# Latent attention and output projection: maxima moved to a rotating bank, first two score groups begun early, output tiles split inside the preceding tile

## The chip, the cores and the metric

The kernel runs on one core of a Trainium2 chip. The metric is the device time of one execution in microseconds (us), as the median of three runs. The core's engines run side by side, each on its own instruction stream in program order: TensorE (PE in the profile, with its weight loads as PEld), VectorE (DVE), ScalarE (ACT), GpSimd (POOL), and SyncE (SP), which here only issues transfers. Engines wait for each other through semaphores. Matrix products land in PSUM, which the program holds as one tile `PB` of eight banks of 128 x 512 words.

## The reference

The reference is a two-layer backbone over 1,024 latent tokens and 256 context tokens with model width 1,024. Layer 0 is windowed attention, layer 1 is latent attention, and a final RMS norm gives the output. The change touches only the end of layer 1:

```
s = (einsum("bqhd,bkhd->bhqk", qn, kn) + einsum("bqhd,bkd->bhqk", qr, kr)) * scale
p = softmax(s, axis=-1)
o = einsum("bhqk,bkhd->bqhd", p, v)          # 16 heads, 64 values each
yx = (o * silu(gx)) @ w_out                  # 1024 x 1024
x = x + gate_x[:, None] * yx
return rms_norm(x, final_g)
```

Only the 1,024 latent tokens are queries here; the keys are all 1,280 tokens.

## The kernel before

**Units.** Attention runs as 16 units (`UnitB`, numbered 0 to 15 by `ui`): eight pairs of heads, each for two halves of 512 queries. Unit `ui` has pair `ui // 2` and half `ui % 2`. Keys come in ten chunks of 128 (`c` = 0 to 9). All instructions from here to the end are in the order in which the program writes them, on every engine; no scheduler moves them.

**Scores.** `score(c)` makes the transposed scores of both heads of the pair for one chunk: 10 matmuls (five terms, two heads; the two heads of a term sit in different halves of the rows) into banks 3 and 4 for even `c`, 5 and 6 for odd `c`. The fifth term (`KR`, part 1, 36 rows) also adds minus the row maximum: rows 32 to 35 of each head's part of `q[:, 3]` hold it. Then ACT takes the exponential of both banks at once (128 x 1024) into a ring of six buffers, and POOL adds it into the running sum `acc` (in unit 15, from `c` = 5, DVE does that).

**Maxima of the next unit.** While unit `ui` runs, `nu.top(PIECES[c])` makes the untransposed scores of unit `ui + 1` in two banks taken in turn from banks 0, 1, 2 (`topb`), and DVE reduces each bank to maxima. At the unit's end, `turn` reduces these and transposes them on PE into bank 5 (`psd`); `shift` writes them into `q[:, 3]`, one head's rows by DVE and the other's by four ACT instructions.

**Values.** `PV` multiplies exponentials and values into bank 7: chunks 0 to 4 at `c` = 5, chunks 5 to 9 at the unit's end. `fin` copies bank 7 out. `fin2` (the sums of `acc` over partitions, four PE passes into bank 5, copied out by ACT), `fin3(0)`, `fin3(1)` (reciprocal and product for 256 queries each) and `fin4` (times the gate, store to `og_d`) of unit `ui` run inside unit `ui + 1`.

**Fills.** At the end of units 0, 2, ..., 12 `make_K` builds the next pair's keys: three pieces of 6 matmuls (512, 512 and 256 wide), each in the next bank of its own turn over banks 0, 1, 2 (`fillb`), split into a high and a low part by ACT and DVE. At the end of units 3, 7 and 11 `make_V` builds values in five pieces of 12 matmuls of 256. Units 1, 5, 9, 13 and 14 have no fill. So the order at a unit's end is: `PV(5, 10)`, `turn`, the previous unit's `fin3(1)`, `shift`, its `fin4`, the fill, `fin`, and then `score(0)` of the next unit.

**Output projection.** `out_tiles` does eight tiles of 128 tokens. `fetch_out` loads a tile's 1024 x 128 attention outputs from `og_d` and its 128 x 1024 residual. `split` makes a high part (ACT copy, 128 x 1024, L121) and a low part (DVE difference, L122). Then come two groups (`c` = 0, 1) of 8 x 3 matmuls of 128 x 512 (L126, L127, L128: high x high, low x high, high x low), in banks 0 to 3 in turn. After each group DVE multiplies by the gate (L1434) and adds the residual (L1435), and ACT sums squares (L1436). POOL makes the norm factor (L1450 to L1452), DVE applies it to both halves (L1463), and SP stores them. `out_tiles` is a generator: it stops three times inside tile 0, and unit 15's `fin2`, `fin3`, `fin4` are put in after the third stop, in the middle of the second group. Tile `ti + 1` is fetched after the first group of tile `ti` (tile 4 at the end of tile 3), and is split at the head of its own tile.

Of the kernel before, what the change touches and what calls it, by code (L numbers as in the profile page):

```python
# [9 lines left out]
F32 = mybir.dt.float32  # L10
F32R = mybir.dt.float32r
BF16 = mybir.dt.bfloat16
AF = mybir.ActivationFunctionType
# [20 lines left out]
class Ring:  # L34
# [6 lines left out]
    def next(self):  # L41
        b = self.bufs[self.i % len(self.bufs)]
        self.i += 1
        return b


def shp(ap, *dims):
    n = 1
    for d in dims:
        n *= d  # L50
    ap = ap[:, 0:n]
    if len(dims) == 1:
        return ap
    names = "abcdefg"[: len(dims)]
    kw = {c: d for c, d in zip(names[1:], dims[1:])}
    return ap.rearrange("p (" + " ".join(names) + ") -> p " + " ".join(names), **kw)
# [3 lines left out]
def kernel(ctx: ExitStack, tc: tile.TileContext, t, out, dbg=None):  # L60
    nc = tc.nc
# [7 lines left out]
    ident = cpool.tile([128, 128], F32, name="ident")  # L69
# [13 lines left out]
    load = nc.sync.dma_start  # L83
# [35 lines left out]
    def split(hi, lo, src, lo_eng=None):  # L119

        nc.scalar.copy(hi, src)  # L121
        (lo_eng or nc.vector).tensor_sub(lo, src, hi.bitcast(F32))  # L122
# [786 lines left out]
    og = None  # L909
# [366 lines left out]
    class UnitB:  # L1276
# [37 lines left out]

        def turn(self):
            nc.vector.reduce_max(shp(self.mx, 2, 64)[:, :, 32:36], self.mxp, AX.X, negate=True)
            nc.tensor.transpose(psd[0:100, 0:128], self.mx[:, 0:100], ident)

        def shift(self, engs):
            for r, eng in zip((slice(32, 36), slice(96, 100)), engs):  # L1320
                if eng is nc.vector:
                    eng.tensor_tensor(
                        shp(self.q[r, 3], 4, 128), psd[r, 0:128].unsqueeze(1).to_broadcast([4, 4, 128]),
                        ident[r, r].unsqueeze(2).to_broadcast([4, 4, 128]), ALU.mult,
                    )
                else:
                    for b in range(4):
                        o = self.q[r, 3, b * 128 : b * 128 + 128]
                        eng.activation(o, psd[r, 0:128], AF.Copy, scale=ident[r, r.start + b : r.start + b + 1])  # L1329

        def score(self, c):


            q, kt = self.q, self.kt
            cs = slice(c * 128, c * 128 + 128)
            b = 3 + 2 * (c % 2)
            for i, (k, s, sq, n) in enumerate(((kt, 0, 0, 64), (kt, 0, 1, 64), (kt, 1, 0, 64), (KR, 0, 2, 64), (KR, 1, 3, 36))):
                for e in range(2):
                    r = slice(64 * e, 64 * e + n)
                    nc.tensor.matmul(PB[:, b + e, :], k[r, s, cs], q[r, sq], start=i == 0, stop=i == 4)  # L1340
            E = self.E[c] = shp(Er.next(), 2, 512)
            nc.scalar.activation(E, PB[:, b : b + 2, :], AF.Exp)  # L1342
            acc = shp(self.acc, 2, 512)
            eng = nc.vector if self.i == NU - 1 and c > 4 else nc.gpsimd
            if c == 1:
                eng.tensor_add(acc, self.E[0], E)
            elif c:
                eng.tensor_add(acc, acc, E)  # L1348

# [22 lines left out]
            nc.vector.reciprocal(self.rec[:, js], self.rec[:, js])  # L1372
            nc.vector.tensor_mul(self.o[:, js], self.o[:, js], self.rec[:, js])

        def fin4(self):
            nc.vector.tensor_mul(self.o, self.o, self.gt.bitcast(F32))
            load(out=og_d[self.pair, :, self.ts], in_=self.o)


    gx1 = R[:, 0:1024].bitcast(F32)  # L1380
# [27 lines left out]
        load(out=x, in_=x1_d[256 + ti * 128 : 384 + ti * 128, :])  # L1408
        return o, x

    def out_tiles(nxt):
        for ti in range(8):
            ts = slice(ti * 128, ti * 128 + 128)
            o, xi = nxt
            x = yr.next()
            og = shp(ogr1.next(), 2, 8, 128)
            split(og[:, 0], og[:, 1], o.bitcast(F32))
            st = sm_ring()
            css = [slice(c * 512, c * 512 + 512) for c in range(2)]
            for c in range(2):  # L1420
                parts = [css[c]] if ti < 7 or c == 0 else [slice(512, 768), slice(768, 1024)]
                for i, cs in enumerate(parts):
                    n = cs.stop - cs.start
                    ps = pso1()
                    for k in range(8):
                        mm3(
                            ps[:, 0:n], [og[:, s, k, :] for s in range(2)], [WoB[k][:, s, cs] for s in range(2)],
                            k == 0, k == 7,
                        )
                        if ti == 0 and k == 3:  # L1430
                            yield
                    if c == 0 and ti < 7 and ti != 3:
                        nxt = fetch_out(ti + 1)
                    nc.vector.tensor_mul(x[:, cs], ps[:, 0:n], gx1[:, cs])  # L1434
                    nc.vector.tensor_add(x[:, cs], x[:, cs], xi[:, cs])  # L1435
                    nc.scalar.activation(junk1[:, 0:n], x[:, cs], AF.Square, accum_out=st[:, c + i : c + i + 1])  # L1436
                    if ti == 7 and c + i < 2:
                        nc.vector.tensor_mul(x[:, cs], x[:, cs], fg[:, cs])
                    if ti == 7 and c + i == 1:
                        nc.vector.tensor_add(st[:, 0:1], st[:, 0:1], st[:, 1:2])  # L1440
                        nc.vector.tensor_scalar(st[:, 0:1], st[:, 0:1], 1.0 / D, EPS, ALU.mult, ALU.add)
                if ti == 0:
                    yield
            r = st[:, 3:4]
            if ti == 3:
                nxt = fetch_out(4)
            if ti == 7:
                nc.vector.scalar_tensor_tensor(st[:, 2:3], st[:, 2:3], 1.0 / D, st[:, 0:1], ALU.mult, ALU.add)
            else:
                nc.gpsimd.tensor_add(st[:, 2:3], st[:, 0:1], st[:, 1:2])  # L1450
                nc.gpsimd.tensor_scalar(st[:, 2:3], st[:, 2:3], 1.0 / D, EPS, ALU.mult, ALU.add)
            nc.gpsimd.tensor_tensor(r, st[:, 2:3], mhalf, ALU.pow)  # L1452
            if ti == 7:
                nc.vector.tensor_scalar_mul(x[:, 0:512], x[:, 0:512], r)
                load(out=out[ts, 0:512], in_=x[:, 0:512])
                nc.scalar.activation(x[:, 512:768], x[:, 512:768], AF.Copy, scale=r)
                cs = slice(768, 1024)
                nc.vector.scalar_tensor_tensor(x[:, cs], x[:, cs], r, fg[:, cs], ALU.mult, ALU.mult)
                load(out=out[ts, 512:1024], in_=x[:, 512:1024])
                continue  # L1460
            for c in range(2):
                cs = css[c]
                nc.vector.scalar_tensor_tensor(x[:, cs], x[:, cs], r, fg[:, cs], ALU.mult, ALU.mult)  # L1463
                load(out=out[ts, cs], in_=x[:, cs])
# [32 lines left out]
    for ui, u in enumerate(units):  # L1497
        pu = units[ui - 1] if ui else None
        nu = units[ui + 1] if ui + 1 < NU else None
        nnu = units[ui + 2] if ui + 2 < NU else None  # L1500
        for c in range(NT):
            if c == 5:
                if pu:
                    pu.fin2()
                u.PV(0, 5)
                if pu:
                    pu.fin3(0)
                if pu and nu is None:
                    pu.fin3(1)
                    pu.fin4()  # L1510
            u.score(c)
            if nu:
                nu.top(PIECES[c])
            if 0 < ui < 12 and c == 2 or ui == 6 and c == 7 or ui in (12, 13) and c in (2, 7):
                next(wo_fill, None)
            if nu is None and c == 0:
                load2(out=gx1, in_=gate_d[1, 0, :].partition_broadcast(128))
                load2(out=fg, in_=t["final_g"].partition_broadcast(128))
        if nnu:
            nnu.prep()  # L1520
        if nu is None:
            nxt = fetch_out(0)
        u.PV(5, NT)
        if nu:
            nu.turn()
            if pu:
                pu.fin3(1)
            nu.shift((nc.vector, nc.scalar))
            if pu:
                pu.fin4()  # L1530
            fill = make_K(u.pair + 1) if u.half == 0 and u.pair < 7 else iter(())
            if ui % 4 == 3:
                fill = make_V(ui // 4 + 1)
            for _ in fill:
                pass
        u.fin()
    out_fill = out_tiles(nxt)
    next(out_fill)
    next(out_fill)
    next(out_fill)  # L1540
    units[-1].fin2()
    units[-1].fin3(0)
    units[-1].fin3(1)
    units[-1].fin4()
    for _ in out_fill:
        pass
    in_order.__exit__(None, None, None)


# [73 lines left out]
```

## Time and profile before

| | us |
|---|---|
| median of three runs | 1640.3 (1639.24 to 1640.78) |
| the profiled execution | 1641.39 |
| its span, first to last instruction | 1639.5 |
| PE busy | 1541.3 (94%) |
| DVE busy | 1008.0 (61%) |
| POOL busy | 776.3 (47%) |
| ACT busy | 733.7 (45%) |
| mean granted TensorE clock | 0.971 |

The profiled execution lies 1.1 us above the median and its span 1.9 us below its own time. The page cuts the span into 40 slices of 41 us and gives one digit for each: busy tenths, or tenths of the full TensorE clock. A timeline row reads: start, duration, engine, line, operation, output <- inputs, shapes, and in square brackets the idle time of the engine before it with the instruction that ended it. Matmul records overlap, since matmuls are pipelined: the step from one start to the next is the cost of one. A row of the view by windows gives, for one stretch, its length, each engine's busy time with its count of instructions, the granted clock, the share of the transfer engines and GB/s.

### The profile page before, as it was taken

What the parts mean: (1) busy time and instruction counts of PE and PEld (TensorE: products, weight loads), DVE (VectorE), ACT (ScalarE), POOL (GpSimd) and SP (SyncE); (2) the same over time, 40 slices, a digit from 0 to 9 for tenths busy, and PEclk for the clock granted to TensorE, in tenths of its full rate; (3) what the DMA queues carried; (4) which work ended last, traced back from release to release, by engine and by line L of the source; (5) the groups of instructions that cost most, each with busy time, mean ns of one, the idle gap of its engine ahead of it and who ended that gap; (6) DMA issues with size and microseconds to landing.
All of it is one profiled execution on the core that took longest, in us unless ns stands there. A gap on an engine that the chain in (4) does not pass through costs nothing.

```text
span 1639.5 us, 24729 instructions
## 1 busy us (share of the span) xinstructions
PE 1541.3 (94%) x9026; PEld 1196.6 (73%) x9026; DVE 1008.0 (61%) x1886; ACT 733.7 (45%) x1425; POOL 776.3 (47%) x722
## 2 busy tenths in 40 slices
PE   6899999989999999998999999999999999997666
PEld 2788788777888888878887887667667667655555
DVE  2666778637777777778263015676776776873232
ACT  2511221248777777776233322444445445441111
POOL 2653356235453333445164503787787777770000
PEclk8899999989999999999999999999999999998877
DMA  8435544573343333253138514011211211212221
GB/s 305 153 123 177 203 151 145 173 187 118 92 139 101 91 91 91 78 160 113 37 116 291 158 55 119 11 52 43 78 56 43 84 43 58 63 54 94 77 82 60
DMA packets 123698, 178.91 MB, mean 109 GB/s; under 512 B 11692, under 2 KB 71724, under 8 KB 123576
## 3 DMA queue, kind: packets, MB, share of 16 engines
q1 hardware_dynamic: 116296, 166.40, 31.9%
q10 hardware_dynamic: 7280, 10.92, 2.2%
q8 instruction: 71, 1.16, 0.3%
q14 instruction: 51, 0.42, 0.1%
HBM read 131.13 MB, written 46.15 MB: 108 GB/s over the span
## 4 chain that ended last, share of the span: by engine, by line
PE 79%; DVE 6%; issue 5%; POOL 4%; ACT 3%; DMA 2%; POOLq 0%; DVEq 0%; SPq 0%; ACTq 0%
PE PB L127 13%; PE PB L126 13%; PE PB L128 13%; PE PB L1340 11%; PE PB L1355 8%; PE PB L570 5%; PE PB L1305 5%; PE PB L560 4%; PE PB L533 2%; PE PB L534 2%; DVE arena_r L122 1%; PE PB L1366 1%; DVE arena_f L344 1%; PE PB L674 1%; POOL arena_r L122 1%
## 5 line engine op out<-in xcount | busy, mean ns | idle before, releaser
L126 PE MATMUL PB<-arena_r 128*128 128x512 f32 (+2 forms) x1312 | 484.0, 369 | 30.8 <-ACT arena_r L121 27.6
L127 PE MATMUL PB<-arena_r 128*128 128x512 f32 (+2 forms) x1312 | 478.0, 365 | 18.7 <-DVE arena_r L122 15.6
L128 PE MATMUL PB<-arena_r 128*128 128x512 f32 (+2 forms) x1312 | 475.9, 363 | 0.2 <-DVE arena_r L122 0.2
L126 PEld LDWEIGHTS PB<-arena_r 128*128 128x128 f32 x1312 | 255.0, 194 | 80.7 <-ACT arena_r L121 32.0
L1348 POOL TENSOR_TENSOR arena_f<-arena_f 128x1024 f32<-128x1024 f32 x123 | 294.5, 2395 | 25.6 <-ACT arena_f L1342 18.4
L127 PEld LDWEIGHTS PB<-arena_r 128*128 128x128 f32 x1312 | 254.2, 194 | 58.0 <-DVE arena_r L122 19.1
L128 PEld LDWEIGHTS PB<-arena_r 128*128 128x128 f32 x1312 | 254.1, 194 | 36.6 <-DVE arena_r L122 0.4
L1311 DVE TENSOR_REDUCE krF<-PB 128x1 f32<-128x512 f32 (+1 forms) x264 | 167.3, 678 | 109.1 <-PE PB L1305 109.1
L1342 ACT ACTIVATE arena_f<-PB 128x1024 f32<-128x1024 f32 x160 | 164.2, 1027 | 150.3 <-PE PB L1340 147.7
L1340 PE MATMUL PB<-arena_r 64*128 64x512 f32 (+1 forms) x1600 | 220.6, 394 | 3.9 <-ACT arena_r L1329 3.2
L122 POOL TENSOR_TENSOR arena_r<-arena_f,arena_r 128x512 fp32r<-128x512 f32 x96 | 132.2, 1389 | 166.6 <-ACT arena_r L121 157.6
L1340 PEld LDWEIGHTS PB<-arena_r 64*128 64x128 f32 (+1 forms) x1600 | 156.1, 184 | 49.6 <-issue 13.3
L122 DVE TENSOR_TENSOR arena_r<-PB,arena_r 128x512 fp32r<-128x512 f32 (+2 forms) x215 | 140.1, 663 | 76.6 <-ACT arena_r L121 75.0
L540 DVE CUSTOM_DVE_ANT_0 arena_f<-PB,arena_f,small 128x256 f32<-128x256 f32 (+1 forms) x288 | 145.4, 524 | 32.6 <-PE PB L534 25.8
L121 ACT CAST arena_r<-PB 128x512 fp32r<-128x512 f32 (+2 forms) x215 | 120.0, 565 | 55.1 <-PE PB L560 40.8
L1355 PE MATMUL PB<-arena_f 128*64 128x512 f32 x640 | 143.6, 595 | 0.0
L541 ACT ACTIVATE arena_f<-arena_f,small 128x640 f32<-128x640 f32 (+2 forms) x160 | 118.9, 743 | 27.9 <-DVE small L540 26.9
L570 PE MATMUL PB<-arena_r 128*128 128x512 f32 x336 | 121.8, 438 | 4.7 <-ACT arena_f L581 4.1
L344 DVE SCALAR_TENSOR_TENSOR arena_f<-arena_f,small 128x512 f32<-128x512 f32 x98 | 115.0, 1219 | 3.9 <-DMA arena_f<-ada_w 3.5
L1305 PE MATMUL PB<-arena_r 64*128 64x512 f32 (+1 forms) x768 | 107.9, 357 | 0.9 <-DVE arena_r L122 0.9
L560 PE MATMUL PB<-ident,arena_f 128*128 128x128 f32 x672 | 105.7, 274 | 0.4 <-ACT arena_f L541 0.3
L1355 PEld LDWEIGHTS PB<-arena_f 128*64 128x64 f32 x640 | 44.4, 137 | 84.2 <-issue 82.0
(165 smaller groups left out, 1886.0 us busy)
## 6 DMA issues: line engine op xcount, KB each, us to landing
arena_r<-q_d SPq DMA_DIRECT2D x148, 128.0 KB, 2.8
arena_f<-ada_w SPq DMA_DIRECT2D x64, 256.0 KB, 3.5
arena_f<-a_w_in SPq DMA_DIRECT2D x40, 256.0 KB, 3.1
arena_f<-ada_w SPq DMA_DIRECT2D x16, 512.0 KB, 7.6
arena_f<-x SPq DMA_DIRECT2D x16, 512.0 KB, 4.2
q_d<-arena_f SPq DMA_DIRECT2D x16, 512.0 KB, 3.1
qn_d<-arena_f SPq DMA_DIRECT2D x16, 512.0 KB, 5.7
arena_r<-qn_d SPq DMA_DIRECT2D x16, 512.0 KB, 5.6
```

What stands on the lines that cost most here:

```text
L122: (lo_eng or nc.vector).tensor_sub(lo, src, hi.bitcast(F32))
L126: nc.tensor.matmul(o, ah, bh, start=first, stop=False)
L127: nc.tensor.matmul(o, al, bh, start=False, stop=False)
L128: nc.tensor.matmul(o, ah, bl, start=False, stop=last)
L560: nc.tensor.transpose(pt[:, h, :], self.Ps[h][:, ci * 128 : ci * 128 + 128], ident)
L570: nc.tensor.matmul(self.pv, V[:, self.chunks[ci], self.g, :], PT[:, s], start=ci == 0 and s == 0, stop=ci == self.m - 1 and s == 1,)
L1305: nc.tensor.matmul(bank[:, o : o + n], self.q[r, s, bs], k[r, 0, n0 : n0 + n], start=s == 0, stop=s == 2)
L1311: nc.vector.reduce_max(self.mxp[:, e, b : b + 1, i], bank[:, 0:n], AX.X)
L1340: nc.tensor.matmul(PB[:, b + e, :], k[r, s, cs], q[r, sq], start=i == 0, stop=i == 4)
L1342: nc.scalar.activation(E, PB[:, b : b + 2, :], AF.Exp)
L1348: eng.tensor_add(acc, acc, E)
L1355: nc.tensor.matmul(PB[r, 7, :], Vq[:, c, h, :], E[:, e], start=c == 0, stop=c == NT - 1)
```

## The change

1. `turn` no longer writes the transposed maxima to bank 5 but to the next bank of `topb` (`self.pm`), and `shift` reads them there.
2. `score` takes a range of terms. At `c` = 0 the unit issues the first four terms of `score(0)` and of `score(1)`, then `top` of chunk 0, then the last term of `score(0)` with its exponential and sum; at `c` = 1 it issues `top`, then the last term of `score(1)`. From `c` = 2 on the order is as before.
3. In unit 15, `fin4` of unit 14 is done in two halves of 256 queries, each stored on its own. The fetch of output tile 0 follows the first half, that of tile 1 the second.
4. `cut_out` is the split of an output tile, in two halves of 512 columns. Tile 0 is cut before unit 15's `fin`; tile `ti + 1` is cut inside tile `ti`, after its first group, and tile `ti + 2` is fetched right behind.
5. `out_tiles` is now an ordinary function, and unit 15's `fin2`, `fin3`, `fin4` stand ahead of it.

```diff
         def turn(self):
             nc.vector.reduce_max(shp(self.mx, 2, 64)[:, :, 32:36], self.mxp, AX.X, negate=True)
-            nc.tensor.transpose(psd[0:100, 0:128], self.mx[:, 0:100], ident)
+            self.pm = topb()
+            nc.tensor.transpose(self.pm[0:100, 0:128], self.mx[:, 0:100], ident)
...
-        def score(self, c):
+        def score(self, c, i0=0, i1=5):
...
+            terms = ((kt, 0, 0, 64), (kt, 0, 1, 64), (kt, 1, 0, 64), (KR, 0, 2, 64), (KR, 1, 3, 36))
+            for i in range(i0, i1):
+                k, s, sq, n = terms[i]
                 for e in range(2):
                     r = slice(64 * e, 64 * e + n)
                     nc.tensor.matmul(PB[:, b + e, :], k[r, s, cs], q[r, sq], start=i == 0, stop=i == 4)
+            if i1 < 5:
+                return
...
-        def fin4(self):
-            nc.vector.tensor_mul(self.o, self.o, self.gt.bitcast(F32))
-            load(out=og_d[self.pair, :, self.ts], in_=self.o)
+        def fin4(self, c0=0, c1=512):
+            cs = slice(c0, c1)
+            nc.vector.tensor_mul(self.o[:, cs], self.o[:, cs], self.gt[:, cs].bitcast(F32))
+            t0 = self.ts.start
+            load(out=og_d[self.pair, :, t0 + c0 : t0 + c1], in_=self.o[:, cs])
...
+    def cut_out(f, eng=None):
+        o, x = f
+        og = shp(ogr1.next(), 2, 8, 128)
+        for h in range(2):
+            hs = slice(4 * h, 4 * h + 4)
+            split(og[:, 0, hs], og[:, 1, hs], o[:, hs].bitcast(F32), eng)
+        return og, x
...
-    def out_tiles(nxt):
+    def out_tiles(ready, got):
         for ti in range(8):
             ts = slice(ti * 128, ti * 128 + 128)
-            o, xi = nxt
+            og, xi = ready
             x = yr.next()
-            og = shp(ogr1.next(), 2, 8, 128)
-            split(og[:, 0], og[:, 1], o.bitcast(F32))
...
-                        if ti == 0 and k == 3:
-                            yield
-                    if c == 0 and ti < 7 and ti != 3:
-                        nxt = fetch_out(ti + 1)
+                    if c == 0 and ti < 7:
+                        ready = cut_out(got)
+                        if ti < 6:
+                            got = fetch_out(ti + 2)
...
                 if pu and nu is None:
+                    pu.fin4(0, 256)
+                    first = fetch_out(0)
                     pu.fin3(1)
-                    pu.fin4()
-            u.score(c)
+                    pu.fin4(256, 512)
+                    got = fetch_out(1)
+            if c == 0:
+                u.score(0, 0, 4)
+                u.score(1, 0, 4)
+            if c > 1:
+                u.score(c)
             if nu:
                 nu.top(PIECES[c])
+            if c < 2:
+                u.score(c, 4, 5)
...
-        if nu is None:
-            nxt = fetch_out(0)
         u.PV(5, NT)
...
+        else:
+            ready = cut_out(first)
         u.fin()
-    out_fill = out_tiles(nxt)
-    next(out_fill)
-    next(out_fill)
-    next(out_fill)
-    units[-1].fin2()
-    units[-1].fin3(0)
-    units[-1].fin3(1)
-    units[-1].fin4()
-    for _ in out_fill:
-        pass
+    u.fin2()
+    u.fin3(0)
+    u.fin3(1)
+    u.fin4()
+    out_tiles(ready, got)
```

More of the change, by code (lines that the diff above doesn't have):

```diff
@@ L1322, in shift @@
                     eng.tensor_tensor(
-                        shp(self.q[r, 3], 4, 128), psd[r, 0:128].unsqueeze(1).to_broadcast([4, 4, 128]),
+                        shp(self.q[r, 3], 4, 128), self.pm[r, 0:128].unsqueeze(1).to_broadcast([4, 4, 128]),
                         ident[r, r].unsqueeze(2).to_broadcast([4, 4, 128]), ALU.mult,
@@ L1328, in shift @@
                         o = self.q[r, 3, b * 128 : b * 128 + 128]
-                        eng.activation(o, psd[r, 0:128], AF.Copy, scale=ident[r, r.start + b : r.start + b + 1])
-        def score(self, c):
+                        eng.activation(o, self.pm[r, 0:128], AF.Copy, scale=ident[r, r.start + b : r.start + b + 1])
+        def score(self, c, i0=0, i1=5):
             q, kt = self.q, self.kt
@@ L1336, in score @@
             b = 3 + 2 * (c % 2)
-            for i, (k, s, sq, n) in enumerate(((kt, 0, 0, 64), (kt, 0, 1, 64), (kt, 1, 0, 64), (KR, 0, 2, 64), (KR, 1, 3, 36))):
+            terms = ((kt, 0, 0, 64), (kt, 0, 1, 64), (kt, 1, 0, 64), (KR, 0, 2, 64), (KR, 1, 3, 36))
+            for i in range(i0, i1):
+                k, s, sq, n = terms[i]
                 for e in range(2):
@@ L1441, in out_tiles @@
                         nc.vector.tensor_scalar(st[:, 0:1], st[:, 0:1], 1.0 / D, EPS, ALU.mult, ALU.add)
-                if ti == 0:
-                    yield
             r = st[:, 3:4]
-            if ti == 3:
-                nxt = fetch_out(4)
             if ti == 7:
```

## The prediction

> **What bounds the kernel now.** I read the page's slices first, then windows by stage, then who waited for whom on PE, then timelines.
>
> ```profile
> span 1639.5 us, 24729 instructions
> ...
> PEclk8899999989999999999999999999999999998877
> ```
>
> ```profile
> 742.70:745.00 2.30, 0.18 (x2) 0.13 (x2) 2.30 (x6) 1.56 (x5) 1.29 (x3) 1.00 0.42 110
> 745.00:750.00 5.00, 3.50 (x27) 3.27 (x28) 4.15 (x7) 4.16 (x11) 4.26 (x5) 1.00 0.24 52
> 1200.00:1300.00 100.00, 99.81 (x727) 69.73 (x724) 72.36 (x94) 48.76 (x67) 74.76 (x34) 1.00 0.17 52
> 1497.40:1516.70 19.30, 14.35 (x48) 10.93 (x48) 5.01 (x7) 2.38 (x5) 0.93 (x3) 0.73 0.29 96
> 1612.50:1632.70 20.20, 14.96 (x72) 12.51 (x72) 7.39 (x13) 2.89 (x7) 0.93 (x3) 0.75 0.07 27
> 1632.70:1639.50 6.80, 0.00 (x0) 0.00 (x0) 1.89 (x5) 1.02 (x3) 0.55 (x1) 0.67 0.21 77
> ```
>
> The clock row shows the tail at once: its last four slices of 41 us read 8, 8, 7, 7. The windows give busy time of PE, PEld, DVE, ACT, POOL, then the granted clock, the transfer share and GB/s. In the units (1200 to 1300) PE is busy all the time at full clock, so whatever makes PE wait there is paid. In the output projection it is not: a tile of 48 matmuls takes 19.3 us (the last one 20.2) at a granted clock of 0.73 to 0.75. The next two views, PE's waits in the tail and then in the units, say for what:
>
> ```profile
> PE PB L126 <- ACT arena_r L121: 25.5, 7, 5.9
> PE PB L127 <- DVE arena_r L122: 14.8, 7, 2.3
> ```
>
> ```profile
> PE PB L1340 <- ACT arena_r L1329: 3.2, 5, 0.7
> PE PB L1340 <- DVE arena_r L1322: 0.5, 1, 0.5
> ```
>
> The tail loses 40.3 us in waits for the split of each tile, seven times both halves. The units lose 3.7 us to the shift, at the five boundaries without a fill. The timeline of one change of tile, PE, then DVE, then ACT:
>
> ```profile
> 1511.55 0.39 PE L128 MATMUL PB<-arena_r 128*128 128x512 f32 x1
> ...
> 1516.31 0.39 PE L128 MATMUL PB<-arena_r 128*128 128x512 f32 x1
> 1519.95 0.80 PE L126 MATMUL PB<-arena_r 128*128 128x512 f32 x1 [3.26 <-ACT arena_r L121]
> 1522.78 0.79 PE L127 MATMUL PB<-arena_r 128*128 128x512 f32 x1 [2.03 <-DVE arena_r L122]
> 1523.38 0.63 PE L128 MATMUL PB<-arena_r 128*128 128x512 f32 x1
> 1523.80 0.63 PE L126 MATMUL PB<-arena_r 128*128 128x512 f32 x1
> ```
>
> ```profile
> 1516.73 0.69 DVE L1434 TENSOR_TENSOR arena_f<-PB,arena_r 128x512 f32<-128x512 f32 x1 [4.02 <-PE PB L128]
> 1517.46 0.69 DVE L1435 TENSOR_TENSOR arena_f<-arena_f,arena_r 128x512 f32<-128x512 f32 x1
> 1520.18 1.41 DVE L1463 SCALAR_TENSOR_TENSOR arena_f<-arena_f,small 128x512 f32<-128x512 f32 x2 [2.03 <-POOL small L1452]
> 1521.51 1.22 DVE L122 TENSOR_TENSOR arena_r<-arena_r 128x1024 fp32r<-128x1024 f32 x1
> ```
>
> ```profile
> 1518.87 1.03 ACT L121 CAST arena_r<-arena_r 128x1024 fp32r<-128x1024 f32 x1
> ```
>
> The split is late by order alone: ACT's copy stands behind the preceding tile's square sum, DVE's difference behind its L1463, which waits for POOL. From 1511.55 to 1516.31 are 21 matmuls, 0.227 us each. After the gap a matmul costs 0.42 (1523.38 to 1523.80): PE pays the idle time, then a spell at half clock.
>
> **The tail, step by step.** The split moves into the preceding tile, ahead of that tile's L1434. A tile of 48 x 0.227 = 10.9 us must now cover, on DVE, the difference (1.22), L1434 and L1435 twice (2.8), L1463 (1.41), 5.4 in all, and one stretch of about 2 us in which DVE waits for POOL. In order, tile t's L1463 ends about 5.3 us into tile t + 1 (1516.31 to 1521.59 by these rows), the next differences by 6.5, and their tile begins at 10.9: 4 us are left, so I cost the moved split (as two halves, four instructions instead of two, some 0.1 us more) at nothing; without that cover it would cost the 2 us per tile that PE now waits for L122. The fetch moves a tile earlier. On SP it stands ahead of the stores of its own tile and behind those of the preceding one, which wait for the same L1463 at 5.3 us; it has more than a tile to land. Its buffers (two for outputs, three for residuals, two for splits) were last read a tile before.
>
> What stands ahead of tile 0 (PE, then DVE):
>
> ```profile
> 1474.69 4.51 PE L1355 MATMUL PB<-arena_f 128*64 128x512 f32 x20
> ...
> 1490.37 1.08 PE L1366 MATMUL PB<-arena_f,small 128*64 128x512 f32 x4
> 1491.38 0.50 PE L126 MATMUL PB<-arena_r 128*128 128x512 f32 x1
> ```
>
> ```profile
> 1470.76 6.54 DVE L1348 TENSOR_TENSOR arena_f<-arena_f 128x1024 f32<-128x1024 f32 x5
> ```
>
> The last values end at 1474.69 + 4.51 = 1479.2. The `fin2` matmuls come next: 1.0 us (1490.37 to 1491.38), and the sums they read are done by 1477.3. Tile 0's split needs ACT after the last exponential and DVE after 1477.3, plus 1.22: 1478.5, or about 1479 since `fin4` in halves and two queued fetches delay DVE's start slightly. Both are ready before 1480.2, when tile 0 begins. The two half stores add one transfer, and SP waits longer between them, with only the gate load behind. Unit 15's `fin3` and `fin4` on DVE then run beside tile 0, and tile 4 is fetched only in tile 2, so its store is long done.
>
> Then 384 matmuls x 0.227 = 87 us without a gap: 1567.2. Behind the last one stand 0.2 us of its own and the 6.8 of the last window, which the change doesn't touch: 1574.3. The tail gives 1639.5 - 1574.3 = 65 us: some 41 of waits, the rest half clock.
>
> **The units, step by step.** A boundary with a K fill (unit 10 to 11), as PE, ACT, PEld, DVE:
>
> ```profile
> 1332.23 0.48 PE L126 MATMUL PB<-arena_r 128*128 128x512 f32 x1
> ```
>
> ```profile
> 1333.30 1.12 ACT L1329 ACTIVATE arena_r<-PB,ident 4x128 fp32r<-4x128 f32 x4 [4.84 <-DVE arena_r L1322]
> ...
> 1337.43 1.03 ACT L1342 ACTIVATE arena_f<-PB 128x1024 f32<-128x1024 f32 x1 [0.59 <-PE PB L1340]
> ```
>
> ```profile
> 1335.87 1.01 PEld L1340 LDWEIGHTS PB<-arena_r 64*128 64x128 f32 x10
> 1336.91 0.47 PEld L1305 LDWEIGHTS PB<-arena_r 64*128 64x128 f32 x4
> 1337.38 1.13 PEld L1340 LDWEIGHTS PB<-arena_r 64*128 64x128 f32 x10
> 1338.52 0.45 PEld L1305 LDWEIGHTS PB<-arena_r 64*128 64x128 f32 x4
> 1338.99 1.13 PEld L1340 LDWEIGHTS PB<-arena_r 64*128 64x128 f32 x10
> ```
>
> ```profile
> 1337.80 1.29 DVE L1311 TENSOR_REDUCE krF<-PB 128x1 f32<-128x512 f32 x2 [0.85 <-PE PB L1305]
> ```
>
> *The maxima's bank: a new wait.* A unit takes 20 + 1 = 21 banks from `topb`, a multiple of three, so the maxima always stand in bank 0, which the fills use too, until the shift's ACT part has read them (1333.30 + 1.12 = 1334.4). The built order shows that wait, for DVE and ACT, on one fill matmul at each of the ten fills. `fillb` has made 8 calls before unit 0's fill, so the pieces go to banks 2, 0, 1 in units 0, 2, 3 and 12; to 1, 2, 0 in 4, 6, 7; to 0, 1, 2 in 8, 10, 11. Where bank 0 comes first, PE stands from 1332.2 to 1334.4 with the whole fill and the next unit behind it: 2.2 us, three times, 6.6. Where it comes second, a piece of 6 x 0.227 = 1.4 us goes first: 0.8, four times, 3.2. Third: nothing. Sum 9.8; the bounds are 6 (a shorter shift) and 14 (DVE is held at some boundaries by `fin3(1)`).
>
> *The last term's place: a later exponential.* Before, score 0's five pairs begin at 1335.87, the exponential at 1337.43, 0.75 us after the fifth pair's start at 1336.68, and score 2, which reuses its banks, at 1338.99, 3.12 us after score 0. Now eight pairs and two of `top` stand ahead of the last term: it starts at about 2.17 us, the exponential at 2.92, ending at 3.95, so score 2 waits until 4.0: 0.88 lost. The second `top` shares a bank with the first and now follows it by one pair: the first of DVE's two reductions (1.29 for both, begun 0.66 after the second pair) ends at 3.3, then about 0.6 of PE work: also 3.9 to 4.0, under the same wait. PE is busy throughout, so nothing gives this back: ten boundaries with a fill and unit 0's start, 11 x 0.88 = 9.7, less some 0.7 where the first `top` waited anyhow: 9. Bounds 0 (if the banks came free sooner) and 13.
>
> *What the reorder removes.* The 3.7 us of waits for the shift go; but there too score 2 now waits for an exponential begun at 2.9 us, where it began at about the same time before. I take 0; bounds 0 and -3.7.
>
> Sum: -65 + 9.8 + 9 = -46. On the span, 1593.5; the profiled execution took 1641.4, 1.1 above the median, so the median goes from 1640.3 to 1594.
>
> The new stalls could also cost clock. The rows speak against it: a gap of 2.1 us at 742.7 left the granted clock at 1.00, while the tail's idle 3.26 + 2.03, with one matmul between, brought 0.73. In "TensorE: Matmul & The Clock Gate" of the Trainium skill, "HAM oscillation" says no idle gap above about 3.4 us, which fits these rows and adds nothing to the sum; "A second HAM failure mode: psum-queue depth-cycling" of the same page says that short idles between groups cycling through banks can make the clock oscillate too, which would add up to 5.2 us per boundary and is a rival below.
>
> **Rivals.**
> 1. *The units lose little* (0.12): the exponential's start or the bank wait is partly covered. For it: both are worked out from single boundaries. Against it: PE idles nowhere else in the units. With a loss of 5 instead of 19: 1580.
> 2. *The splits stay late* (0.08): DVE's order paces the tiles. 2 us on each of seven, as the wait for L122 now: 14, so 1608. Against it: 4 us of slack.
> 3. *The clock falls at the long stalls* (0.06): (1 - 0.73) x 2 x 19.3 = 10.4 us at half clock per drop, so up to 5.2 lost; at units 8, 10, 11 alone 15.6: 1610.
> 4. *Slower* (0.03): the clock falls at every boundary with a fill: ten drops of 5.2 are 52, so 1646. It decides from nine drops on (46 / 5.2). Against it: the 2.1 us row above.
>
> **How the numbers follow.** The forecast, 1594, has 0.71; its own range is 1587 to 1602. Leaving out no more than 2 in 10, the range reaches from most of rival 1 to rival 2: 1580 to 1608. A change under 0.2% (3.3 us) can't be told from none: faster 0.96, same 0.01 (a few drops short of rival 4), slower 0.03.
>
> **What would show it.** Right: PE's waits for L121 and L122 in the tail near zero, granted clock 1.00 to the end, a tile every 10.9 us; new waits of L126 for the shift (2.2 us three times, 0.8 four times); PE waiting about 0.9 us for the exponential ahead of score 2. Wrong: the tail's waits stay, PE waits there for `fetch_out`'s transfers, or the granted clock falls inside the units.

## The result, and the profile after

The changed kernel takes 1595.0 us (median of four executions, 1593.15 to 1597.22), the kernel before beside it 1640.5 us: a ratio of 0.9719, 95% interval 0.9697 to 0.9741. The forecast was 1594. From the page of the changed kernel, its span and the granted clock in 40 slices:

```profile
span 1594.1 us, 24753 instructions
...
PEclk8899999999999999999999999999999999999999
```

The four low slices at the end are gone. Windows of the changed kernel, two stretches inside the output projection (busy time of PE, PEld, DVE, ACT, POOL, granted clock, transfer share, GB/s):

```profile
1520.00:1540.00 20.00, 20.00 (x90) 16.56 (x89) 10.52 (x16) 4.23 (x10) 1.87 (x6) 1.00 0.40 134
1540.00:1560.00 20.00, 20.00 (x90) 16.57 (x89) 8.86 (x15) 4.96 (x12) 1.87 (x6) 1.00 0.40 135
```

PE is busy without a gap at full clock. Its first and last matmul of the projection:

```profile
1499.65 0.50 PE L126 MATMUL PB<-arena_r 128*128 128x512 f32 x1
...
1587.06 0.28 PE L128 MATMUL PB<-arena_r 128*128 128x256 f32 x1
```

The projection takes 87.4 us of PE from the first start to the last, where the kernel before needed 151.5 (1480.95 to 1632.4). PE's waits from 1000 us to the end are now these:

```profile
PE PB L126 <- ACT arena_r L1330: 8.7, 7, 1.9
PE PB L1305 <- DVE krF L1311: 5.8, 15, 1.2
PE PB L1343 <- ACT arena_f L1347: 0.9, 1, 0.9
```

The 40 us of waits for the split (L121, L122) have gone. New are seven waits of a fill's matmul for the shift (L1330), 8.7 us, and fifteen of the second `top` for the maxima's reduction (L1311), one in every unit from 0 to 14. The last row is a wait in unit 15. The boundary of units 8 and 9 shows both, PE first and then PEld:

```profile
1283.61 0.50 PE L126 MATMUL PB<-arena_r 128*128 128x512 f32 x1 [1.93 <-ACT arena_r L1330]
```

```profile
1287.28 1.70 PEld L1343 LDWEIGHTS PB<-arena_r 64*128 64x128 f32 x16
...
1290.62 0.29 PEld L1305 LDWEIGHTS PB<-arena_r 64*128 64x128 f32 x3 [0.75 <-DVE krF L1311]
1290.73 0.41 PEld L1343 LDWEIGHTS PB<-arena_r 36*128 36x128 f32 x2
1291.55 0.99 PEld L1343 LDWEIGHTS PB<-arena_r 64*128 64x128 f32 x10 [0.41 <-ACT arena_f L1347]
```

Score 2 starts 4.27 us after score 0 (1287.28 to 1291.55); in the row of before it was 3.12. At the other boundaries with a fill it is about 4.0, and between the two scores PE waits there only for L1311.

One line of each trace divides a run into stages: the 16 transpositions of the maxima, whose first and last start stand in the row. Between them lie units 0 to 14; from the last one to the end lie unit 15 and the output projection. Before and after:

```profile
L1317 PE MATMUL PB<-ident,krF x16: 270/317/317, 1003.6 to 1454.8; 128*100 128x128 f32 x16
```

```profile
L1318 PE MATMUL PB<-ident,krF x16: 270/316/317, 1003.2 to 1474.6; 128*100 128x128 f32 x16
```

The units went from 451.2 to 471.4 us, 20.2 more. The rest went from 1639.5 - 1454.8 = 184.7 to 1594.1 - 1474.6 = 119.5, 65.2 less.

### The profile page after: what moved, and what is told of

Same layout as the page of the kernel before. It is cut to its first block, busy times and chain, and to the rows that moved or that the text cites. A ratio compares the mean times of both kernels' runs of the same rounds, so it can differ in the third digit from the quotient of the medians.

```text
span 1594.1 us, 24753 instructions
## 1 busy us (share of the span) xinstructions
PE 1524.8 (96%) x9026; PEld 1190.6 (75%) x9026; DVE 1013.6 (64%) x1895; ACT 735.0 (46%) x1433; POOL 775.7 (49%) x722
## 4 chain that ended last, share of the span: by engine, by line
PE 81%; DVE 5%; ACT 4%; DMA 3%; POOL 3%; issue 3%; SPq 0%; POOLq 0%; DVEq 0%; ACTq 0%
PE PB L126 13%; PE PB L127 13%; PE PB L128 13%; PE PB L1343 12%; PE PB L1360 8%; PE PB L1305 5%; PE PB L570 5%; PE PB L560 4%; PE PB L533 2%; PE PB L534 2%; DMA arena_f<-a_w_in 1%; PE PB L1371 1%; DVE arena_f L344 1%; ACT arena_f L581 1%; DVE krF L1311 1%
## 5 line engine op out<-in xcount | busy, mean ns | idle before, releaser
L126 PE MATMUL PB<-arena_r 128*128 128x512 f32 (+2 forms) x1312 | 477.1, 364 | 12.2 <-ACT arena_r L1330 8.7
L127 PE MATMUL PB<-arena_r 128*128 128x512 f32 (+2 forms) x1312 | 470.1, 359 | 3.0 <-POOL arena_r L727 2.1
L128 PE MATMUL PB<-arena_r 128*128 128x512 f32 (+2 forms) x1312 | 469.8, 358 | 0.2 <-DVE arena_r L122 0.2
L1353 POOL TENSOR_TENSOR arena_f<-arena_f 128x1024 f32<-128x1024 f32 x123 | 294.4, 2394 | 19.3 <-ACT arena_f L1347 12.1
L126 PEld LDWEIGHTS PB<-arena_r 128*128 128x128 f32 x1312 | 250.9, 191 | 59.0 <-ACT arena_r L1330 11.2
L127 PEld LDWEIGHTS PB<-arena_r 128*128 128x128 f32 x1312 | 250.5, 191 | 37.8 <-POOL arena_r L727 2.7
L128 PEld LDWEIGHTS PB<-arena_r 128*128 128x128 f32 x1312 | 250.3, 191 | 35.4 <-DVE arena_r L122 0.4
L1311 DVE TENSOR_REDUCE krF<-PB 128x1 f32<-128x512 f32 (+1 forms) x264 | 167.1, 677 | 119.0 <-PE PB L1305 118.4
L1343 PE MATMUL PB<-arena_r 64*128 64x512 f32 (+1 forms) x1600 | 220.7, 395 | 1.0 <-ACT arena_f L1347 0.9
L122 POOL TENSOR_TENSOR arena_r<-arena_f,arena_r 128x512 fp32r<-128x512 f32 x96 | 131.7, 1384 | 167.3 <-ACT arena_r L121 157.3
L122 DVE TENSOR_TENSOR arena_r<-PB,arena_r 128x512 fp32r<-128x512 f32 (+2 forms) x215 | 140.2, 663 | 82.4 <-ACT arena_r L121 81.4
L1343 PEld LDWEIGHTS PB<-arena_r 64*128 64x128 f32 (+1 forms) x1600 | 160.0, 184 | 41.6 <-issue 13.3
L121 ACT CAST arena_r<-PB 128x512 fp32r<-128x512 f32 (+2 forms) x215 | 120.3, 565 | 61.6 <-PE PB L560 39.5
L1305 PE MATMUL PB<-arena_r 64*128 64x512 f32 (+1 forms) x768 | 112.6, 360 | 6.5 <-DVE krF L1311 5.8
L1351 POOL TENSOR_TENSOR arena_f<-arena_f 128x1024 f32<-128x1024 f32 x16 | 38.5, 2403 | 142.9 <-ACT arena_f L1347 142.9
```

What stands on the lines that cost most here:

```text
L126: nc.tensor.matmul(o, ah, bh, start=first, stop=False)
L127: nc.tensor.matmul(o, al, bh, start=False, stop=False)
L128: nc.tensor.matmul(o, ah, bl, start=False, stop=last)
L1305: nc.tensor.matmul(bank[:, o : o + n], self.q[r, s, bs], k[r, 0, n0 : n0 + n], start=s == 0, stop=s == 2)
L1311: nc.vector.reduce_max(self.mxp[:, e, b : b + 1, i], bank[:, 0:n], AX.X)
```

## Experiments

Each ratio below is to the kernel before, run beside that experiment; in the three sets of runs its median was 1641.5, 1641.9 and 1641.8 us.

### The parts alone

The change divides into the output projection's part and the units' part, and the latter into the maxima's bank and the order of the first two scores.

`e1_tail_only` keeps changes 3 to 5 and leaves the units as before:

```diff
-            self.pm = topb()
-            nc.tensor.transpose(self.pm[0:100, 0:128], self.mx[:, 0:100], ident)
+            nc.tensor.transpose(psd[0:100, 0:128], self.mx[:, 0:100], ident)
...
-            if c == 0:
-                u.score(0, 0, 4)
-                u.score(1, 0, 4)
-            if c > 1:
-                u.score(c)
+            u.score(c)
             if nu:
                 nu.top(PIECES[c])
-            if c < 2:
-                u.score(c, 4, 5)
```

> The output projection's part of the change alone; the units as before (maxima in bank 5, score(0) and score(1) whole). Theory: the parts add up, the tail gives 65 us and the units' part costs 20, so 1640 - 65 = 1575. Rival (the early start of the scores pays for part of its cost, so that the units' part as a whole costs under 5 us and the tail gives only some 50): 1590.

1574.6 us, ratio 0.9594 (0.9579 to 0.9608), as the theory had it.

`e2_units_only` is the reverse: changes 1 and 2 on the kernel before.

> The units' part alone, the output projection as before. Theory: 1640 + 20 = 1660, slower than before. Rival (the units' part gains the 3.7 us of shift waits, and its stalls are covered): 1637 to 1640.

1660.4 us, ratio 1.012 (1.0103 to 1.0136). The parts add up to within 2.5 us: -67 and +19, against -45.5 together. The units' part of the change makes the kernel slower, and the gain of the other part hides it.

`e3_order_only` is the changed kernel with the fills' turn over the banks set, so that bank 0 comes last:

```diff
+            fillb.i = 1
             fill = make_K(u.pair + 1) if u.half == 0 and u.pair < 7 else iter(())
```

> The changed kernel, but each fill starts at bank 1, so that its pieces go to banks 1, 2, 0 and bank 0 comes last, 2.7 us after the maxima's transposition. Theory: the wait of the fills for the maxima's bank goes (12 us in the trace, with one spell of half clock behind it), the wait of score 2 for its exponential stays: 1595 - 12 = 1583. Rival (the fills only uncover a shift that something else waits for right behind): 1590 to 1595.

1581.6 us (1581.39 to 1581.74), ratio 0.9636 (0.9622 to 0.9651), 13.4 below the changed kernel. In the trace no wait of PE for L1330 is left; the fifteen waits for L1311 stand as before, 5.8 us.

`e4_bank_only` is the changed kernel with the scores' order as before:

```diff
-            if c == 0:
-                u.score(0, 0, 4)
-                u.score(1, 0, 4)
-            if c > 1:
-                u.score(c)
+            u.score(c)
             if nu:
                 nu.top(PIECES[c])
-            if c < 2:
-                u.score(c, 4, 5)
```

> The changed kernel with score(0) and score(1) whole again, as before the change; the maxima stay in the rotating bank, the fills start where they did. Theory: the wait for the exponential goes (9.5 us), the bank's wait stays, and the 3.7 us of waits for the shift come back: 1595 - 9.5 + 3.7 = 1589. Rival (score 2 waits for the second piece of the maxima's scores, whose bank is not free yet, whatever the order): 1595 to 1599.

1587.6 us, ratio 0.9674 (0.9659 to 0.9688). In its trace no wait for L1311 is left, so the second `top` waits because of the order too. With the tail's part alone as the base, the order costs 1581.6 - 1574.6 = 7.0 us, the bank 13.0, and both 20.5. The stages, from one trace of each, divide it a little otherwise. The rows are those of `e3_order_only`, of `e4_bank_only`, and of the tail's part alone in its second run (`e9_tail_again`, below):

```profile
L1318 PE MATMUL PB<-ident,krF x16: 270/316/317, 1001.3 to 1460.4; 128*100 128x128 f32 x16
```

```profile
L1318 PE MATMUL PB<-ident,krF x16: 270/316/317, 1005.8 to 1467.0; 128*100 128x128 f32 x16
```

```profile
L1317 PE MATMUL PB<-ident,krF x16: 270/317/317, 1003.4 to 1454.7; 128*100 128x128 f32 x16
```

Units 0 to 14 take 459.1, 461.2 and 451.3 us: in the traces the order costs 7.8 and the bank 9.9. (The first trace of the tail's part has 452.9, with a spell of half clock at 1428 us.) The bank's wait of 9.8 in the forecast is thus met; the 13 us between the medians hold about 3 us that these traces don't place. In the changed kernel the two together cost 20.2, which is 2.5 more than their sum; 1.4 of that is the spell of half clock shown below under "The clock at the fills", the rest is not placed.

### The split's place against the early transfer

`e5_split_late` keeps the early fetches and puts each split back at the head of its own tile:

```diff
+        after = None
...
+            if ti:
+                ready = cut_out(got)
+                got = after
             og, xi = ready
...
-                    if c == 0 and ti < 7:
-                        ready = cut_out(got)
-                        if ti < 6:
-                            got = fetch_out(ti + 2)
+                    if c == 0 and ti < 6:
+                        after = fetch_out(ti + 2)
```

> The changed kernel with the transfers as early as in it (tile t + 2 fetched inside tile t), but tile t + 1 split again at the head of its own tile, behind tile t's norm. Theory: the place of the split in ACT's and DVE's order is what mattered; seven gaps come back with their spells of half clock, (19.3 - 10.9) = 8.4 us each, 59 in all: 1595 + 59 = 1654. Rival (the earlier fetch is what helps): 1595 to 1605.

1650.4 us, ratio 1.0051 (1.0036 to 1.0066). PE's waits in the tail are back:

```profile
PE PB L126 <- ACT arena_r L121: 19.8, 7, 2.8
PE PB L127 <- DVE arena_r L122: 14.7, 7, 2.2
```

So of the 55 us that the split's place is worth, 34.5 are waits, and in four of its tiles the granted clock is back at 0.80 to 0.83. The transfers of tiles 1 to 7 were not what PE waited for. The first of the two waits is 2.8 us instead of 3.26, since the copy is in halves and PE starts on the first; that is some 3 us of the 4 by which the expectation was too long.

### What the half clock costs

`e6_warm_gaps` is the kernel before with 22 matmuls per tile, in tiles 1 to 7, whose result nothing reads:

```diff
+            def idle_mm(n):
+                for _ in range(n):
+                    nc.tensor.matmul(PB[:, 4, :], WoB[0][:, 0, 0:128], WoB[0][:, 0, 0:512], start=True, stop=True)
+
+            if ti:
+                idle_mm(14)
...
+                        if ti and c == 0 and k == 0:
+                            nc.tensor.matmul(ps[:, 0:n], og[:, 0, k, :], WoB[k][:, 0, cs], start=True, stop=False)
+                            idle_mm(8)
...
```

> The kernel before, with work added in the output projection that nothing reads: ahead of tiles 1 to 7, 14 matmuls of 128x512 into an unused bank while PE waits for the high part, and 8 more between the first matmul and the second, while it waits for the low part. The waits stay, but PE is hardly idle in them. Theory: the granted clock stays at 1.00, a tile takes 10.9 + 6.0 = 16.9 us instead of 18.4 to 19.9, so seven tiles save some 16 us: 1640 - 16 = 1624, and the half clock's share of the tail's 65 us is about a quarter. Rival (the slow matmuls behind a gap come from the gap itself, not from the clock): 1640 to 1645.

1627.2 us, ratio 0.991 (0.9893 to 0.9926): more work, and 14.7 us faster. Two windows of 17 us, one tile period each in its trace, have the clock at 1.00:

```profile
1537.00:1554.00 17.00, 16.42 (x72) 12.94 (x71) 5.28 (x8) 2.39 (x5) 0.93 (x3) 1.00 0.30 94
1554.00:1571.00 17.00, 16.41 (x71) 12.95 (x70) 5.24 (x8) 2.39 (x5) 0.93 (x3) 1.00 0.29 93
```

The waits are as long as before: from a tile's last matmul to the next tile's first 3.66 us (1532.96 to 1536.62) against 3.64, from that to the tile's second 2.82 against 2.83. So the slow matmuls behind a gap are the granted clock's doing, and about 15 of the tail's 65 us were half clock.

The rest is waits, and a wait costs more than the idle time that the view counts: in the prediction's rows PE takes 6.47 us from 1516.31 to 1522.78 for two steps of 0.227, so 6.0 are lost where 5.3 are counted as idle. Over seven tiles that is some 5 us, an estimate from these rows. Tile 0 of the kernel before waited for its split as well, 1.75 + 0.76 us, ahead of the stretch in which the prediction counted 40.3. Together, 40.3 + 5 + 2.5 + 14.7 place some 62 to 63 of the 65 us.

### The clock at the fills

In the trace of the changed kernel the fill of unit 11 waits 1.93 us like those of units 8 and 10, but then runs at half speed. Windows ahead of, in and behind that spell:

```profile
1375.00:1378.20 3.20, 1.27 (x9) 0.90 (x8) 2.57 (x3) 1.12 (x4) 2.39 (x1) 1.00 0.06 15
1378.20:1381.60 3.40, 3.40 (x18) 3.40 (x17) 0.00 (x0) 0.59 (x1) 0.00 (x0) 0.50 0.44 131
1381.60:1385.00 3.40, 3.40 (x30) 3.40 (x29) 0.00 (x0) 1.21 (x3) 0.00 (x0) 1.00 0.29 105
```

In 3.4 us at clock 0.50 PE ran 18 of these matmuls, against 30 right behind: 12 x 0.12 = 1.4 us lost, with 0.12 us as the step of these matmuls of 256 at full clock.

`e7_long_shift` makes the wait longer:

```diff
-            nu.shift((nc.vector, nc.scalar))
+            nu.shift((nc.scalar, nc.scalar))
```

> The changed kernel with both heads' rows of the shift written by ACT (eight instructions of 0.28 us) instead of one head's by DVE. The fill's wait for the maxima's bank grows from 1.9 to about 2.8 us of idle time at units 8, 10 and 11, and from 0.5 to about 1.4 at units 0, 2, 3. Theory (a spell of 3.4 us at half clock follows where a gap fills more than about half of one of the windows of 3.4 us in which the clock is set): two or three of the three long gaps, instead of one, are followed by such a spell, and the time is 5 to 10 us above the changed kernel's. Rival (only gaps above 3.4 us lower the clock, and the spell seen at unit 11 has another cause): no more than one spell, 4 to 6 us above.

1596.3 us, from a single execution. I had sized the edit wrongly: four ACT instructions (1.12 us) take the place of DVE's 0.68, so the long waits grew to 2.33 us only, 10.7 in all instead of 8.7. One of the three was followed by a spell (again unit 11). That doesn't tell the theories apart.

Traces of the other kernels do better. The waits of 1.93 us stand in the traces of the changed kernel, `e2_units_only`, `e4_bank_only` and `e5_split_late`, three in each; 1, 1, 0 and 2 of them were followed by a spell of half clock. So half clock follows a wait of 1.93 us in some executions, at 4 of 12 waits here. That it depends on how the wait falls into periods of 3.4 us in which the clock is set would fit the spells' lengths (3.4 us here, 6.8 at about 743 us in `e2_units_only` and at 747 in `e8_mixed`), but this was only argued.

### A version that takes the good half

`e8_mixed` has the output projection's part, the fills from bank 1 on, and the early scores only in the five units that follow a unit without a fill:

```diff
+            early = ui in (2, 6, 10, 14, 15)
-            if c == 0:
+            if early and c == 0:
                 u.score(0, 0, 4)
                 u.score(1, 0, 4)
-            if c > 1:
+            if c > 1 or not early:
                 u.score(c)
             if nu:
                 nu.top(PIECES[c])
-            if c < 2:
+            if early and c < 2:
                 u.score(c, 4, 5)
...
+            fillb.i = 1
             fill = make_K(u.pair + 1) if u.half == 0 and u.pair < 7 else iter(())
```

> The output projection's part; the early start of score(0) and score(1) only in units 2, 6, 10, 14 and 15, which follow a unit without a fill; in all others score(0) and score(1) whole; maxima in the rotating bank, fills from bank 1 on. Theory: at the five boundaries without a fill the early start costs nothing and takes away the 3.7 us of waits for the shift, behind which a spell of half clock followed at unit 13 in the trace of the tail's part alone; so the lowest time of that kernel, 1572.7, in nearly every run: 1572 to 1573. Rival (the shift's waits cost nothing beyond themselves): 1574 to 1576, as the tail's part alone.

1573.8 us (1571.57 to 1575.99), ratio 0.9585 (0.9572 to 0.9598). Beside it on the same chip, the tail's part alone:

> The output projection's part alone once more, beside the mixed kernel on the same chip. Theory: 1574.5, scattered over 1572.5 to 1577 as in its first runs, since the half clock follows the shift's waits in some executions only. Rival (its scatter came from the chip of the first runs): within 0.5 us of the mixed kernel, and as little scattered.

1575.6 us (1574.33 to 1578.48), ratio 0.9597 (0.9584 to 0.961). Both are faster than the kernel before and the changed kernel; which of the two is the faster is not settled, since the intervals overlap. In units 0 to 14 the mixed kernel gains 1.2 us (450.1 against 451.3): PE's waits there went only from 3.8 us (3.2 + 0.4 + 0.2) to 2.1, since the second `top` waits instead:

```profile
PE PB L1305 <- DVE krF L1311: 2.1, 4, 1.2
```

My reason for a steadier time did not hold: the mixed kernel scatters over 4.4 us, though its trace has no half clock in the units. The scatter comes from ahead of them as well, where all these kernels have the same code: the first transposition starts at 1000.8 us in the trace of `e2_units_only` and at 1005.8 in that of `e4_bank_only`. What makes this difference stays open. Half clock between 640 and 1000 us does not explain it: the first of these traces has a spell of 6.8 us there, the second none.

## Why the prediction was right, point by point

- **The tail, 65 us less: right.** 65.2 by the stages. A tile is paced by PE alone (87.4 us for all eight against 87), and the 4 us of slack in DVE's order held: in the changed kernel PE waits for no split. `e5_split_late` shows that the place in the engines' order did it. The division into 41 us of waits and some 24 of half clock was off: filling the gaps gave back 14.7 us, and the waits cost more than their idle time.
- **Ready before tile 0: right, but closer than forecast.** I had the split of tile 0 ready about 1.2 us before PE needs it. DVE finished the second half at 1498.51 + 1.29 = 1499.8, after tile 0 had begun at 1499.65. These are DVE's and ACT's rows of the changed kernel:

```profile
1492.06 6.53 DVE L1353 TENSOR_TENSOR arena_f<-arena_f 128x1024 f32<-128x1024 f32 x5
1498.51 1.29 DVE L122 TENSOR_TENSOR arena_r<-arena_r 128x512 fp32r<-128x512 f32 x2
```

```profile
1496.97 1.14 ACT L121 CAST arena_r<-arena_r 128x512 fp32r<-128x512 f32 x2 [1.43 <-DMA arena_r<-og_d]
```

  ACT's copy waited 1.43 us for the transfer of `og_d`, but it ended at 1498.11; DVE came to the difference at 1498.51, right behind its own sums (L1353). PE lost nothing. I had counted the halves only as a cost; they give PE the first half earlier. Whether they were needed was not tried: a whole difference of 1.22 us, begun at 1498.51, would have ended at 1499.73, and the first matmul that reads the low part starts at 1500.00.
- **The maxima's bank, 9.8 us: right**, 9.9 by the stages. The waits are 1.93 us at the three fills where bank 0 comes first (forecast 2.2). Where it comes second they are 0.5 in units 0, 2 and 3 and 1.4 in unit 12 (forecast 0.8): in unit 12 DVE's part of the shift came late, behind `fin3(1)`, 1.2 us after the transposition's start (1414.67 against 1413.49) where it was 0.4 in unit 8. The forecast had this as the reason of its upper bound.
- **The later exponential, 9 us: nearly right in size, 7.8 by the stages, but PE waited at the other end.** The prediction put two ends at 3.9 to 4.0 us after score 0, the exponential and the bank of the second `top`, and named the exponential. In the changed kernel it is at the second `top` that PE stands, waiting for DVE's reduction: 0.75 to 0.82 us on PEld in units 0 to 13, 1.47 in unit 14. For the exponential PE waits in unit 9 alone of these (0.41, shown above). So the sign that I had named, 0.9 us of waiting for the exponential ahead of score 2, is not what showed. The two ends do fall together: in unit 11 the exponential ends at 1350.88 + 1.03 = 1351.91, and score 2 starts at 1351.96. What would be left with one of them removed was not tried.
- **No gain from the shift's waits: nearly right.** The mixed kernel gets 1.2 us of the 3.7.
- **Rival 3, the clock at the long stalls: its mechanism is real, my argument against it was not.** I had held a row against it in which a 2.1 us gap at 742.7 us left the clock at 1.00. The same place in the trace of `e3_order_only`:

```profile
739.00:743.50 4.50, 2.38 (x18) 2.17 (x18) 4.50 (x8) 3.76 (x9) 2.82 (x4) 1.00 0.39 120
743.50:746.90 3.40, 3.07 (x14) 2.72 (x13) 3.01 (x4) 2.90 (x8) 3.23 (x3) 0.50 0.19 39
```

  Six of the eleven traces of this study have a spell at 0.50 there; one row was one throw. A granted clock that falls inside the units was one of the signs of being wrong; it fell once there, at unit 11. What kept the forecast whole is the price: a spell of 3.4 us cost 1.4 us in the rows of unit 11 and 1.6 between the two traces of the tail's part (452.9 and 451.3 us for units 0 to 14), not the 5.2 that I took from the tail's rows, and it follows only some of the stalls.
- **Rivals 1, 2 and 4** didn't occur: the units lost 20.2 us against a forecast of 18.8, no split was late, and the clock did not fall at every fill.
- **The sum** came out within about 1 us, and some of that is luck: the order cost 1.2 us less than forecast, and the two parts of the units together 2.5 us more than their sum.

## What to carry to other kernels

Put the preparation of the next tile where the in-order engines are idle in the present one, and count each engine's order over a whole period: here the place of two instructions was worth 55 us, of which a good part is half clock behind the gaps. When something small is moved into a rotating buffer, work out whose turn meets it: the counts of calls gave 9.8 us in advance, and one line that sets the turn avoids the wait. And starting work early helps only if what releases the next steps doesn't move back with it: here the exponential did, and the second `top` came upon a bank that was still being read, so that a part of the change that looks like hiding a wait costs 8 us.

## What the runs showed of the hardware

Half clock can follow a single wait of about 2 us: one of 1.93 us in 4 of 12 cases, one of about 2.1 us in 6 of 11. The tail has two waits in a row, 3.26 and 2.03 us. In "TensorE: Matmul & The Clock Gate" of the Trainium skill, "HAM oscillation" puts the limit at idle gaps of about 3.4 us; the measurement decides, and here about 2 us is enough in some executions. The prediction's remark that this rule fits its rows holds only if the tail's two waits, with one matmul between them, count as one. In the trace of `e1_tail_only` even less idle time was followed by a spell:

```profile
1425.15:1428.56 3.41, 2.31 (x15) 1.34 (x15) 3.35 (x3) 1.71 (x5) 3.05 (x2) 1.00 0.00 0
1428.56:1431.97 3.41, 3.41 (x20) 2.71 (x17) 1.75 (x4) 1.59 (x2) 0.00 (x0) 0.50 0.45 154
```

PE was busy for 2.31 of 3.41 us, with matmuls of 64 rows mostly and two waits of 0.45 and 0.65 us, and 3.4 us at half clock followed. What "A second HAM failure mode: psum-queue depth-cycling" of the same page of the Trainium skill says, that short idles between groups of matmuls suffice, fits that better. Why these 1.1 us of idle time sufficed, and whether the rows in use count, stays open.
